# A two-batch encoder layer on one core: block products in another order, mixture tiles loaded by the sync engine, row splits behind the mixture, accumulating stores over two stages

## The chip, the cores and the metric

The kernel runs on one core of one Trainium2 chip. The core has a matrix engine (TensorE, in the profile PE, with its weight loads as PEld), a vector engine (VectorE, DVE), an activation engine (ScalarE, ACT), a general engine (GpSimd, POOL) and a sync engine (SyncE, SP) that here only issues transfers. GpSimd issues transfers as well. Each engine runs its own instructions strictly in the order in which they were written out for it, and each waits on semaphores for what the others and the transfers deliver. The metric is the device time of one execution in microseconds (us), as the median of the runs.

## The reference

One layer of an encoder is applied to two requests with the same weights: `x_prompt` with 1024 tokens (A in what follows) and `x_sample` with 512 tokens (B), 1024 wide.

```python
h = rms_norm(x, pre_w)
cols = jnp.einsum('bsd,dc->bsc', h, w_in)
m_qk, m_v, m_o, m_z, m_i, m_f, a_qkv, a_z, gate = jnp.split(cols, np.cumsum(IN_SPLITS)[:-1], axis=-1)
y_m = mlstm_mixer(m_qk, m_v, m_o, ...) * jax.nn.silu(m_z)
y_a = dilated_attention(a_qkv, rel_table) * jax.nn.silu(a_z)
p_m = jnp.einsum('bsc,cd->bsd', y_m, w_pm)
p_a = jnp.einsum('bsc,cd->bsd', y_a, w_pa)
g = jax.nn.sigmoid(gate).reshape(b_, s_, N_BRANCHES, D_MODEL)
merged = g[:, :, 0] * p_m + g[:, :, 1] * p_a
out = jnp.einsum('bsd,de->bse', merged, w_out)
return x + rms_norm(out, post_w)
```

`dilated_attention` computes three groups of windows and mixes them for every token and head by their softmax denominators. This is the mixture that the change speaks of:

```python
mx = jnp.stack(maxes)
w = jnp.exp(mx - jnp.max(mx, axis=0))
num = jnp.einsum('gbsh,gbshe->bshe', w, jnp.stack(outs))
den = jnp.sum(w * jnp.stack(dens), axis=0)
return (num / den[..., None]).reshape(b_, s_, A_WIDTH)
```

## The kernel before

All large products are in float32. Each operand is split into a rounded high part and the low part that is left (the high part by a copy on ScalarE, the low part by a subtraction on VectorE), and each product is three matmuls: high by high, low by high, high by low. That is `mm3` (L232 to L237), and its three lines are L235, L236 and L237. A split thus costs two instructions on two engines, and a matmul can start only when both halves are there.

**The first stage.** A's input projection uses one level of Strassen-Winograd: instead of eight block products, seven, on sums and differences of the blocks. `unit_pair` (L835) does this for a pair of units (a unit is 128 columns of the projection): the seven products `m1` to `m7` of twelve matmuls each, and between them copies on ScalarE and sums on VectorE. Every product has a bank of PSUM of its own (the pool hands out tiles named `d`), but for two: `m2` accumulates onto `m1`'s bank and `m3` onto `m5`'s. Before `m2` may start, ScalarE must have copied `m1` to `u2` (L854, in the trace `pu<-d`); before `m3` may start, ScalarE must have copied `m5` to `q[1][1]` (L863, in the trace `c<-d`). The sums of the weights' blocks are split into halves by `pair_split` (L762 to L769), high on ScalarE (L766), low on VectorE (L767), into the tiles `phla` and `phlb`; two of the splits, `s3, a22` and `s4`, are made inside `unit_pair`, and `s3` is the weight of `m7`.

**The middle.** Behind it come A's mLSTM and attention with the short pieces of B's projection woven in, then A's output (`outputs`). Its last stage does not add to the result in memory by itself: it puts 16 stores on a list `adds`; each is a transfer issued by GpSimd that accumulates onto `T.y` in memory (L2496, `y_prompt<-H`). B's attention (`attend`) runs at the end of this part; it writes its outputs with their maxima and denominators to `og` in memory.

**The tail** is about B alone. Five pieces take part, and TensorE's order there is the order in which they are written out: the mixture `combine` is a generator that is stepped between the steps of a `Fill`, which hands out weights and runs `branches` and then `final`.

- `combine` (L2066): the four tiles of 128 tokens go through two buffers, tiles 0 and 2 through `V0a`, tiles 1 and 3 through `V1a`. For each tile a load from `og` per group (three), then on VectorE `weigh` (L2081 to L2096, which gives the weights `cw`, with reciprocal L2094), three products `mix` (L2103) and two sums `add` (L2109); then `turn` (L2111): four transposes on TensorE (L2114) and a multiplication by `az` on VectorE (L2116). Tiles 0 to 2 are then stored to `ym` in memory; the last tile goes directly into the operands of `proj_a` (L2120). The loads of tiles 2 and 3 are issued by `ahead` on `self.side`, which is GpSimd's queue there, and stand behind `self.loaded`, the last load of weights.
- `split` (L2196): loads the four rows 8 to 11 of `ym` (tiles 0 to 2 side by side, 384 wide) through the three buffers `self.rows_in` (`ymr`, `ymr`, `sraw`), and splits each, high L2211 on ScalarE into `H`, low L2212 on VectorE into `K`. The fourth row uses the buffer of the first.
- `branches` (L2562): `proj_m` makes eight column tiles of eight steps of three matmuls, evicted by VectorE (L2593) into `V0b` and `V1b`, and issues the accumulating stores, two per column tile (L2583 to L2585); `proj_a` makes eight column tiles of four steps, and merges each with its `proj_m` tile (L2612 to L2615). It is `proj_a` that needs `H` and `K`.
- `final` (L2634): 192 matmuls with `w_out`. Its weights come through two buffers `wraw` (loaded by L288) and are split by L299 on ScalarE and L305 on VectorE into places that `more_places` adds to.
- `STEPS` and `fill.stage` set how many of the Fill's steps lie between two steps of `combine`.

**What sets the order.** TensorE's order in the tail, and SP's, is that of the code (`manual_schedule`). The order on VectorE, ScalarE and GpSimd is set by a scheduler at build time, which takes the instruction that its own timeline finds ready first. `issue_after(x.ins)` keeps an instruction behind `x` in that order, and `high_priority` pulls one ahead. The mixture's own VectorE steps have both (they stay behind the last eviction of `proj_m` and behind the sums of the tile before); `split`'s low parts have neither.

## Time and profile before

| | |
|---|---|
| runs (us) | 2201.39, 2202.01, 2204.64; median 2202.01 |
| the profiled execution (us) | 2203.76 |
| its span, first to last instruction (us) | 2202.0 |
| mean granted TensorE clock | 0.995 |
| moved by the transfers | 469.04 MB, mean 213 GB/s |
| matmuls | 11530 |

The profile is of one execution. A row of a group names the engine, the line of the code, the operation, the output and input tiles, and their shape; "x608" is the count. The busy time, the mean duration and the idle time that the engine spent ahead of these instructions follow, with what ended it. "PE tp <- DVE Q" reads: TensorE waited to write `tp` until VectorE had made `Q`. Rows of the timeline begin with the start in us from the span's beginning. Matmuls are pipelined: one takes 0.39 us or so from start to end, but the next starts 0.227 us after it, so that TensorE's busy time hides waits shorter than the overlap.

### The profile page before, as it was taken

The page shows a single profiled execution, that of the slowest core. Times are in us where ns is not written, and L with a number is a line of the kernel's source. Part 1 is how long each engine was busy: PE and PEld are TensorE (multiplying, and loading weights), DVE is VectorE, ACT ScalarE, POOL GpSimd, SP SyncE. Part 2 cuts the span into 40 slices and gives each one's busy share as a digit, 9 for nine tenths or more (in the row PEclk, how much of TensorE's full clock was granted, in tenths as well). Part 3 has the DMA queues.
Part 4 walks back from the last instruction along what each step waited for, and adds up shares of the span by engine and source line. Part 5 has one row for each costly group of instructions (what it writes and reads, how often), then busy time and mean ns, then how long its engine had stood idle before and what let it go on. Part 6 is the DMA issues. An engine that isn't in the chain of part 4 may idle for free.

```text
span 2202.0 us, 33824 instructions
## 1 busy us (share of the span) xinstructions
PE 2164.1 (98%) x11530; PEld 1840.2 (84%) x11530; DVE 1502.4 (68%) x2923; ACT 1122.2 (51%) x2324; POOL 808.2 (37%) x1050
## 2 busy tenths in 40 slices
PE   9999999999999999999999999999999999999978
PEld 8988888888888788888888889998788888888766
DVE  8766675668888776537888775574667846676844
ACT  7322354455444444446777666666755544435312
POOL 1000444333234775325776650011045532322431
PEclk9999999999999999999999999999999999999989
DMA  5642687955555554358646558877668788986873
GB/s 213 192 138 72 210 274 242 302 203 201 184 185 196 200 201 153 134 201 267 197 161 232 170 169 263 239 238 196 201 233 283 239 278 295 319 253 196 251 234 107
DMA packets 234134, 469.04 MB, mean 213 GB/s; under 512 B 38281, under 2 KB 120393, under 8 KB 233834
## 3 DMA queue, kind: packets, MB, share of 16 engines
q1 hardware_dynamic: 199736, 343.81, 47.8%
q0 software_dynamic: 30624, 110.48, 15.6%
q10 hardware_dynamic: 3602, 12.59, 1.4%
q8 instruction: 91, 1.49, 0.3%
q14 instruction: 81, 0.66, 0.1%
HBM read 314.56 MB, written 156.43 MB: 214 GB/s over the span
## 4 chain that ended last, share of the span: by engine, by line
PE 81%; DVE 5%; DMA 5%; issue 4%; ACT 3%; POOL 1%; DVEq 0%; SPq 0%; POOLq 0%; ACTq 0%
PE d L235 11%; PE dense L235 11%; PE d L237 11%; PE d L236 11%; PE dense L236 11%; PE dense L237 11%; PE lg L1851 2%; PE pt L1881 1%; DVE pwk L882 1%; PE o L1924 1%; PE num L235 1%; PE num L237 1%; PE num L236 1%; PE num L1544 1%; DMA wraw<-w_out 1%
## 5 line engine op out<-in xcount | busy, mean ns | idle before, releaser
L235 PE MATMUL dense<-H,wh 128*128 128x512 f32 x712 | 288.9, 406 | 0.0
L237 PE MATMUL dense<-H,wl 128*128 128x512 f32 x712 | 279.4, 392 | 0.0
L236 PE MATMUL dense<-H,wh 128*128 128x512 f32 x664 | 260.3, 392 | 0.0
L235 PE MATMUL d<-Hh,phla 128*128 128x512 f32 x608 | 237.7, 391 | 1.9 <-ACT pu L854 1.6
L237 PE MATMUL d<-Hh,phla 128*128 128x512 f32 x608 | 236.7, 389 | 0.0
L236 PE MATMUL d<-Hl,phla 128*128 128x512 f32 x608 | 236.6, 389 | 0.0
L235 PE MATMUL d<-Hh,phlb 128*128 128x512 f32 x456 | 177.8, 390 | 0.9 <-ACT c L863 0.9
L236 PE MATMUL d<-Hl,phlb 128*128 128x512 f32 x456 | 177.4, 389 | 0.0
L237 PE MATMUL d<-Hh,phlb 128*128 128x512 f32 x456 | 177.4, 389 | 0.0
L237 PEld LDWEIGHTS dense<-H,wl 128*128 128x128 f32 x712 | 134.0, 188 | 30.1
L235 PEld LDWEIGHTS dense<-H,wh 128*128 128x128 f32 x712 | 134.5, 189 | 18.0 <-issue 0.9
L305 DVE TENSOR_TENSOR wl<-wraw,wh 128x1024 fp32r<-128x1024 f32 (+1 forms) x96 | 120.0, 1252 | 30.2 <-ACT wh L299 30.1
L785 POOL TENSOR_TENSOR psum_w<-pw_raw 128x512 f32<-128x512 f32 x38 | 52.7, 1387 | 235.5 <-DMA pw_raw<-w_in 127.5
L235 PEld LDWEIGHTS d<-Hh,phla 128*128 128x128 f32 x608 | 114.1, 188 | 29.3 <-ACT pu L854 5.8
L1870 DVE CUSTOM_DVE_ANT_0 ls<-lg,bias 128x256 f32<-128x256 f32 (+2 forms) x240 | 78.6, 350 | 86.8 <-PE lg L1851 65.8
L236 PEld LDWEIGHTS dense<-H,wh 128*128 128x128 f32 x664 | 125.3, 189 | 14.5
L237 PEld LDWEIGHTS d<-Hh,phla 128*128 128x128 f32 x608 | 114.1, 188 | 23.9
L236 PEld LDWEIGHTS d<-Hl,phla 128*128 128x128 f32 x608 | 114.1, 188 | 23.4
L1874 ACT ACTIVATE ls<-ls,nm 128x256 f32<-128x256 f32 (+1 forms) x192 | 87.4, 456 | 77.4 <-DVE nm L1872 58.7
L299 ACT ACTIVATE wh<-wraw 128x1024 fp32r<-128x1024 f32 (+1 forms) x99 | 101.7, 1031 | 45.2 <-PE dense L236 23.4
L235 PE MATMUL d<-v,Hh 128*128 128x484 f32 (+1 forms) x336 | 121.3, 361 | 0.1
L237 PE MATMUL d<-v,Hl 128*128 128x484 f32 (+1 forms) x336 | 120.6, 359 | 0.4 <-DVE Hl L475 0.4
(749 smaller groups left out, 5936.2 us busy)
## 6 DMA issues: line engine op xcount, KB each, us to landing
pw_raw<-w_in SPq DMA_DIRECT2D x76, 512.0 KB, 4.6
wraw<-w_in SPq DMA_DIRECT2D x63, 512.0 KB, 4.7
pw_raw<-w_q SPq DMA_DIRECT2D x44, 512.0 KB, 6.5
pre<-phlb SPq DMA_DIRECT2D x32, 512.0 KB, 4.9
aqk_a<-pwk SPq DMA_DIRECT2D x32, 512.0 KB, 7.5
pre<-phlb SPq DMA_DIRECT2D x16, 1024.0 KB, 7.8
wh<-pre POOLq DMA_DIRECT2D x27, 512.0 KB, 6.4
wl<-pre POOLq DMA_DIRECT2D x27, 512.0 KB, 6.4
```

The costliest lines, as they stand in the source:

```text
L235: nc.tensor.matmul(out, lh, rh, start=start, stop=False, **kw)
L236: nc.tensor.matmul(out, lh, rl, start=False, stop=False, **kw)
L237: nc.tensor.matmul(out, ll, rh, start=False, stop=stop, **kw)
L299: high = nc.scalar.activation(hi[:, :n], raw[:, :n], AF.Copy)
L305: low = (self.lows or nc.vector).tensor_sub(lo[:, :n], raw[:, :n], hi[:, :n].bitcast(F32))
L785: self.nc.gpsimd.tensor_add(s[:, 0], ws[1][:, 0], ws[1][:, 1])
L882: nc.vector.scalar_tensor_tensor(y, raw[:, i:i + S], cw[:, i:i + 1], y, op0=OP.mult, op1=OP.add)
L1544: nc.tensor.matmul(pn, hi[:, j], z[:, c1], start=j == 0 and z is v[0], stop=False)
L1851: nc.tensor.matmul(lg[:, hh], q[hh][:, qs], z.rearrange("p (n j) -> p n j", j=P)[:, pair], start=z is k[hh], stop=z is not k[hh])
L1870: nc.vector.tensor_tensor_reduce(out=ls[rows, hh], in0=ts["lg"][hh][rows, of], in1=bt[rows, hh, by], scale=1.0, scalar=NEG, op0=OP.add, op ...
L1874: self.held = self.held[-3:] + [nc.scalar.activation(ls[:, hh], ls[:, hh], AF.Exp, bias=nm[:, hh:hh + 1], accum_out=ot[:, 128 + hh:129 + hh])]
L1881: nc.tensor.transpose(pp[:, hh * nk + x], ts["ls"][:, hh, x * P:(x + 1) * P], self.ident)
```

## The change

It has four parts.

1. In `unit_pair` the seven products come in another order: `m1, m6, m7, m5, m2, m4, m3` in place of `m1, m6, m2, m7, m5, m4, m3`. ScalarE's copy of `m5` is gone; VectorE adds `u3` and `m5` straight from PSUM. The priority of the copy `u2` is gone too.
2. In `combine` the loads of tiles 2 and 3 are issued by SP (the default of `fetch`) and no longer stand behind the last load of weights. `az` stays on GpSimd's queue. The last sum of each tile is also kept as `self.summed`; the first tile gets one more step, and the Fill's steps are dealt out by `STEPS` 20, 56 in place of 26, 50.
3. In `split` the low parts stand behind `self.summed`, the latest sum of the mixture when they are written out, which is that of the last tile.
4. In `branches` the sixteen accumulating stores are issued as follows: in `proj_m` two in each of the column tiles 0 and 1 and one in each of 2 to 5, in `proj_a` one in each of its eight. The extra places for split weights are added at column tile 0 of `proj_a` and not at 2, and they lie in `V0a` and `V1a` in place of `H0` and `H3`.

```diff
         m1 = product(B11, a11)
-        with self.tc.high_priority():
-            nc.scalar.activation(u2, m1, AF.Copy)
+        nc.scalar.activation(u2, m1, AF.Copy)
         m6 = product(T2, s2)
         nc.vector.tensor_add(u2, u2, m6)
-        m2 = product(B21, a12, m1)
-        nc.scalar.activation(q[0][0], m2, AF.Copy)
         m7 = product(T3, s3)
         nc.vector.tensor_sub(u3, u2, m7)
         m5 = product(T1, s1)
-        with self.tc.high_priority():
-            nc.scalar.activation(q[1][1], m5, AF.Copy)
-        nc.vector.tensor_add(q[1][1], q[1][1], u3)
+        nc.vector.tensor_add(q[1][1], u3, m5)
+        m2 = product(B21, a12, m1)
+        nc.scalar.activation(q[0][0], m2, AF.Copy)
         m4 = product(T4, a22)
...
         def ahead(t, g=None):
             if t < T.n:
+                if g is not None:
+                    self.fetch(("og", T.S), cs[t % 2][:, g], T.og[t * P:(t + 1) * P, g])
+                    return
                 with self.tc.issue_after(self.loaded.ins):
-                    if g is None:
-                        az[t] = az_of()
...
-                    else:
-                        self.fetch(("og", T.S), cs[t % 2][:, g], T.og[t * P:(t + 1) * P, g], self.side)
+                    az[t] = az_of()
...
                     if i == 5:
-                        summed = last
+                        summed = self.summed = last
...
                     yield
+                    if not t:
+                        yield
                     if t:
                         ahead(t + 1, 2)
...
                     nc.scalar.activation(hi[:, z, :w], t[:, :w], AF.Copy)
-                    nc.vector.tensor_sub(lo[:, z, :w], t[:, :w], hi[:, z, :w].bitcast(F32))
+                    with self.tc.issue_after(self.summed.ins):
+                        nc.vector.tensor_sub(lo[:, z, :w], t[:, :w], hi[:, z, :w].bitcast(F32))
...
+        def accumulate():
+            with self.tc.issue_after(self.loaded.ins):
+                self.adds.pop(0)()
...
-                    if k % 4 == 3 and self.adds:
-                        with self.tc.issue_after(self.loaded.ins):
-                            self.adds.pop(0)()
+                    if k == 3 and ct < 6 or k == 7 and ct < 2:
+                        accumulate()
...
-                if ct == 2:
-                    self.more_places(weights.__self__, [[z[:, 1024 * i:1024 * (i + 1)] for i in range(2)] for z in map(self.take, ("H0", "H3"))])
+                if ct == 0:
+                    self.more_places(weights.__self__, [[z[:, 1024 * i:1024 * (i + 1)] for i in range(2)] for z in map(self.take, ("V0a", "V1a"))])
+                accumulate()
                 pa = self.dense()
...
-STEPS = (316, 260, 192, (6.25, 4.75), 26, 50)
+STEPS = (316, 260, 192, (6.25, 4.75), 20, 56)
...
-                fill.stage(STEPS[5], 3 * B.n + 2)
+                fill.stage(STEPS[5], 3 * B.n + 3)
```

The first place is on VectorE, in the tail, where the last tile of the mixture is worked on. The rows L2094 and L2096 are the end of its weights `cw` (`wd` is the denominators' part), L2103 its products and L2109 its sums in `Q`, L2116 and L2120 what follows its turn, and L2212 the low parts of the rows of `split`. Before:

```order
L2094 RECIPROCAL wd_20671<-wd_20671 128x8
L2212 TENSOR_TENSOR K_20500<-ymr_17723,H_20499 128x384
L2096 SCALAR_TENSOR_TENSOR cw_20666<-cw_20666,wd_20671 128x24
L2212 TENSOR_TENSOR K_20500<-sraw,H_20499 128x384
L2103 TENSOR_TENSOR Q_20303<-V1a,cw_20666 128x512 x3
L2212 TENSOR_TENSOR K_20500<-ymr_17722,H_20499 128x384
L2109 TENSOR_TENSOR Q_20303<-Q_20303 128x512 x2
L2212 TENSOR_TENSOR K_20500<-ymr_17723,H_20499 128x384
L2116 TENSOR_TENSOR az_20298<-tp_20764,az_20298 128x512
L2120 TENSOR_TENSOR K_20500<-az_20298,H_20499 128x4x128
```

After, where the same steps stand at L2091, L2093, L2100, L2106, L2113 and L2117, and L2595 is the eviction of a column tile of `proj_m`:

```order
L2091 RECIPROCAL wd_20626<-wd_20626 128x8
L2093 SCALAR_TENSOR_TENSOR cw_20621<-cw_20621,wd_20626 128x24
L2100 TENSOR_TENSOR Q_20265<-V1a,cw_20621 128x512 x3
L2106 TENSOR_TENSOR Q_20265<-Q_20265 128x512
L2595 SCALAR_TENSOR_TENSOR V1b<-gab,dense 128x512
L2106 TENSOR_TENSOR Q_20265<-Q_20265 128x512
L2113 TENSOR_TENSOR az_20260<-tp_20723,az_20260 128x512
L2595 SCALAR_TENSOR_TENSOR V1b<-gab,dense 128x512
L2117 TENSOR_TENSOR K_20462<-az_20260,H_20461 128x4x128
L2212 TENSOR_TENSOR K_20462<-ymr_17685,H_20461 128x384
L2212 TENSOR_TENSOR K_20462<-sraw,H_20461 128x384
L2212 TENSOR_TENSOR K_20462<-ymr_17684,H_20461 128x384
```

The four low parts stood one ahead of each step of the last tile; now all four come behind its last step (the fourth is two rows further down), and an eviction stands between its two sums.

The second place is on GpSimd, where `proj_m` ends and `proj_a` begins. `y_prompt<-H` are the accumulating stores, `gab` the merge gates, `wh` and `wl` the weights of `proj_a` (split beforehand), `wraw<-w_out` the weights of `final`. Before:

```order
L2496 DMA y_prompt<-H_19609 128x512
L2496 DMA y_prompt<-H_20046 128x512
L276 DMA gab<-gt_b 128x512
L832 DMA wh_7389<-pre 128x1024
L832 DMA wl_7390<-pre 128x1024
L288 DMA wraw_7383<-w_out 128x1024
L288 DMA wraw_7384<-w_out 128x1024
L276 DMA gab<-gt_b 128x512 x3
L288 DMA wraw_7383<-w_out 128x1024
```

After:

```order
L832 DMA wh_7351<-pre 128x1024
L832 DMA wl_7352<-pre 128x1024
L288 DMA wraw_7345<-w_out 128x1024
L2496 DMA y_prompt<-H_19571 128x512
L2496 DMA y_prompt<-H_20008 128x512
L288 DMA wraw_7346<-w_out 128x1024
L276 DMA gab<-gt_b 128x512 x3
L288 DMA wraw_7345<-w_out 128x1024
L2496 DMA y_prompt<-H_19571 128x512
```

The last stores stood ahead of the weights of `proj_a` and of all loads of `w_out`; now eight of them stand among the loads of `w_out`, two ahead of a load. The loads `V0a<-og_b` and `V1a<-og_b`, three each, are no longer on GpSimd's list; they stand on SP's, behind the first tiles' loads and ahead of the first store `ym_b<-az`.

On TensorE the turns of tiles 0 and 1 stand six and three matmuls earlier among those of `proj_m`, and the turns of tiles 2 and 3 where they were. In the first stage ScalarE's list loses the 38 copies of L863.

More of the change, by code (lines that the diff above doesn't have):

```diff
@@ L2127, in ahead @@
             if t < T.n:
+                if g is not None:
+                    self.fetch(("og", T.S), cs[t % 2][:, g], T.og[t * P:(t + 1) * P, g])
+                    return
                 with self.tc.issue_after(self.loaded.ins):
-                    if g is None:
-                        az[t] = az_of()
-                        self.fetch(("az", T.S), az[t].rearrange("p (c s) -> p c s", c=4),
-                                   T.az[:, :, t * P:(t + 1) * P].rearrange("c p s -> p c s"), self.side)
-                    else:
-                        self.fetch(("og", T.S), cs[t % 2][:, g], T.og[t * P:(t + 1) * P, g], self.side)
+                    az[t] = az_of()
+                    self.fetch(("az", T.S), az[t].rearrange("p (c s) -> p c s", c=4),
+                               T.az[:, :, t * P:(t + 1) * P].rearrange("c p s -> p c s"), self.side)
         if slow:
@@ L2591, in proj_m @@
                     if k == KT - 1:
-                        assert ct < KT - 1 or not self.adds
                         self.evicted = nc.vector.scalar_tensor_tensor(m2[ct // 4][:, ct % 4], gates.pop((1, ct)), 1.0, pm, op0=OP.add, op1=OP.mult)
```

## The prediction

> **What bounds the kernel now.** I read the page first: its first part, and its two groups of matmuls of the first stage.
>
> ```profile
> span 2202.0 us, 33824 instructions
> PE 2164.1 (98%) x11530; PEld 1840.2 (84%) x11530; DVE 1502.4 (68%) x2923; ACT 1122.2 (51%) x2324; POOL 808.2 (37%) x1050
> L235 PE MATMUL d<-Hh,phla 128*128 128x512 f32 x608 | 237.7, 391 | 1.9 <-ACT pu L854 1.6
> L235 PE MATMUL d<-Hh,phlb 128*128 128x512 f32 x456 | 177.8, 390 | 0.9 <-ACT c L863 0.9
> ```
>
> TensorE works 2164.1 of 2202.0 us. No matmul is added or taken away, so the change can win only what TensorE waits, or what it runs slowly. Next I asked for the windows of the stages that the diff touches: the length, busy time per engine with counts in brackets, then granted clock, DMA share, GB/s.
>
> ```profile
> 232.00:962.00 730.00, 727.20 (x3194) 597.83 (x3193) 509.37 (x468) 353.35 (x412) 319.47 (x236) 1.00 0.59 202
> 2038.00:2126.00 88.00, 71.49 (x299) 57.62 (x299) 53.94 (x109) 19.68 (x38) 35.62 (x51) 0.90 0.81 229
> 2126.00:2148.00 22.00, 22.00 (x98) 18.12 (x97) 15.52 (x22) 7.62 (x10) 7.49 (x14) 1.00 0.83 279
> 2126.00:2202.00 76.00, 66.71 (x288) 53.48 (x286) 36.62 (x53) 18.49 (x32) 15.07 (x28) 0.97 0.46 157
> ```
>
> The first row is the stage of `unit_pair`: 2.8 us idle in 730. The second runs from B's last attention tile to the end of `proj_m`: 16.5 us idle in 88, clock 0.90. Here is the prize. The third is `proj_a`: not idle. In the fourth most idle time is the drain after the last matmul, which the diff leaves alone. What TensorE waited for in the second window, from the list of waits (total, times, longest):
>
> ```profile
> PE tp L2114 <- DVE Q L2109: 12.2, 1, 12.2
> PE tp L2114 <- DVE cw L2086: 2.2, 2, 2.0
> PE tp L2114 <- DVE X L2109: 2.1, 1, 2.1
> PE dense L235 <- ACT K L2614: 0.8, 1, 0.8
> ```
>
> All but the last are the transposes in `turn`, one set of four for each mixture tile 0 to 3, and the 12.2 us belong to tile 3. Why VectorE was late shows in its timeline (start, length, line, output and inputs, idle before and who ended it).
>
> ```profile
> 2075.31 1.89 DVE L2103 TENSOR_TENSOR Q<-V1a,cw 128x512 f32<-128x512 f32 x3
> 2087.45 0.68 DVE L2109 TENSOR_TENSOR X<-X 128x512 f32<-128x512 f32 x1
> 2094.47 0.17 DVE L2086 TENSOR_TENSOR cw<-V1a 128x8 f32<-128x8 f32 x1 [4.61 <-DMA V1a<-og_b]
> 2096.54 0.20 DVE L2094 RECIPROCAL wd<-wd 128x8 f32<-128x8 f32 x1
> 2105.37 0.56 DVE L2212 TENSOR_TENSOR K<-ymr,H 128x384 fp32r<-128x384 f32 x1 [8.63 <-ACT H L2211]
> 2106.41 1.89 DVE L2103 TENSOR_TENSOR Q<-V1a,cw 128x512 f32<-128x512 f32 x3
> ```
>
> Two delays are in series. Tile 3 is in V1a only at 2094.47. Then, with the weights all but done at 2096.74, VectorE's next instruction in order is a low part of `split` (L2212), whose row isn't there: it stands 8.63 us, and the last products of the mixture stand behind it. The chain says what that row waited for:
>
> ```profile
> 2089.89 7.07 DMA ym_b<-Q
> 2097.10 7.61 DMA ymr<-ym_b
> 2110.24 1.08 PE tp L2114 x4
> 2111.32 0.43 PE dense L235
> ```
>
> Tile 2's result goes to memory in 7.07 us and comes back as a row in 7.61. So tile 3 waits for a round trip of tile 2 that it does not need.
>
> **The mixture.** With `issue_after(self.summed.ins)` all four low parts come behind tile 3's sums on VectorE, as the order rows in the section on the change show. The 8.63 us go. The other delay is the load: POOL issued it late, behind accumulating stores and other loads.
>
> ```profile
> 2084.95 0.57 POOL L276 DMA_DIRECT2D V1a<-og_b  x1
> ```
>
> V1a was free at 2077.20, when tile 1's products ended (2075.31 + 1.89). SP has nothing queued there but the loads and stores of `ym`, so it will issue tile 3 as each group frees, from about 2076. The time from issue to landing is in the list of DMAs, 7.1 us for the same buffer issued by SP (last column):
>
> ```profile
> q0 software_dynamic: 8413, 25.56, 53.7%
> q1 hardware_dynamic: 4864, 5.83, 10.2%
> y_prompt<-H POOLq DMA_DIRECT2D x12, 256.0 KB, 7.9
> V1a<-og_b SPq DMA_DIRECT2D x3, 264.0 KB, 7.1
> wraw<-w_out POOLq DMA_DIRECT2D x8, 512.0 KB, 3.7
> ```
>
> So tile 3 lands by about 2084.3, ahead of tile 2's end on VectorE (2087.45 + 0.68 = 2088.13), and what VectorE does becomes the bound: weights 2.27 (2094.47 to 2096.74), products 1.89, two sums of 0.68, and two instructions that the new order puts between them, an eviction of `proj_m` and the multiplication after tile 2's turn, about 0.7 each. That is 2088.13 + 6.9 = 2095.0. TensorE gets to the turn at the end of the second row below:
>
> ```profile
> 2088.27 0.63 PE L2114 MATMUL tp<-ident,X 128*128 128x128 f32 x4 [2.08 <-DVE X L2109]
> 2097.66 0.39 PE L237 MATMUL dense<-K,wl 128*128 128x512 f32 x1
> 2116.22 0.40 PE L235 MATMUL dense<-H,wh 128*128 128x512 f32 x1
> ```
>
> 2098.05 is 3 us later than 2095.0: no wait is left, 12.2 us go. The other turns stay where they are: turns 0 and 1 move two and one steps ahead in TensorE's order, but what they wait for on VectorE (splits of weights, the stores' normalisations) moves no more than that; I take 0 for their 4.3 us, with all of it as the bound of gain.
>
> The idle time also cost speed. Two windows of the clock:
>
> ```profile
> 2088.00:2092.00 4.00, 3.73 (x12) 3.04 (x13) 1.86 (x3) 0.00 (x0) 1.08 (x2) 0.61 1.10 263
> 2110.00:2116.00 6.00, 5.76 (x16) 4.73 (x17) 2.63 (x5) 0.63 (x1) 2.24 (x5) 0.50 0.17 31
> ```
>
> After the long wait (second row) the clock is 0.50. The transposes took 1.08 instead of 0.63, and from 2111.32 to 2116.22 matmuls start 0.43 apart instead of 0.227 (19.04 us for 84, below): 4.9 us for what takes 2.6. 0.45 + 2.3 = 2.8 us, which go with the wait. Sum for the mixture: 12.2 + 2.8 = 15.0 us. The Trainium skill, page "TensorE: Matmul & The Clock Gate", section "Part 1: The HAM clock gate (the "warmup" mystery)", says that the clock halves after an idle window of about 3.4 us and is given back after about 3.4 us of work. By that alone the slow part would be worth 1.7 us and the sum 13.9; the trace has about 6 us at 0.50, and a dip to 0.61 after a wait of 2.08 that the rule would not throttle, so the rows decide.
>
> The four low parts now come later. The rows arrive at 2104.71 as before (2097.10 + 7.61), as no row shows tile 2's store coming sooner. Of the 342 matmuls behind turn 3, 288 are those of `proj_a` and `final`, so `proj_a` needs the rows after 54: 2098.05 + 0.6 + 54 x 0.227 = 2110.9, and the fourth row 9 matmuls later, at 2113.0. This row's buffer holds the first row until its split has read it, to about 2105.9; a second load of 7.61 and 1.1 for the two halves end at 2114.6, 1.6 too late. But the share of the DMA engines was 0.17 from 2110 on (second row above). I take 0, with 1.6 as the bound.
>
> **The first stage.** Per pair of units seven products of twelve matmuls. Before, the third product goes onto the first one's bank and so waits for the copy u2 (L854), and the seventh onto the fifth's, waiting for the copy at L863. After, four products lie between m1 and m2 on one bank; m5's bank has two products between, and its reader is VectorE. What these waits cost is measured by the products' starts:
>
> ```profile
> 231.99 0.40 PE L235 MATMUL d<-Hh,phla 128*128 128x512 f32 x1
> 719.68 0.50 PE L235 MATMUL d<-Hh,phla 128*128 128x512 f32 x1 [1.57 <-ACT pu L854]
> 771.50 0.39 PE L235 MATMUL d<-Hh,phla 128*128 128x512 f32 x1
> 790.54 0.39 PE L235 MATMUL d<-Hh,phla 128*128 128x512 f32 x1
> 961.68 0.39 PE L237 MATMUL d<-Hh,phlb 128*128 128x512 f32 x1
> ```
>
> An undisturbed pair takes 790.54 - 771.50 = 19.04. There are 38 ((608 + 456) / 28). The stage took 961.91 - 231.99 = 729.9, 6.4 more than 38 x 19.04 = 723.5. That is the most that can be had; the idle columns show only 2.8 of it, since matmuls overlap. It does not all come: at 719.68, the worst, m7 takes the waiting product's slot at 718.1, but its weights are split only at 718.90:
>
> ```profile
> 716.97 1.93 DVE L767 TENSOR_TENSOR phlb<-pw_raw,phlb 128x1024 fp32r<-128x1024 f32 x1
> ```
>
> That leaves 0.8 there, and other pairs have 1 to 3 us to spare for the same split, which moves 2.7 nearer. VectorE's copy of m5 must follow m7's difference, in a stage where VectorE is 70% busy. I take 4.0, with 0 and 6.4 as ends. The 38 copies of L863 that ScalarE no longer makes are worth nothing by themselves: it is busy 353 of 730.
>
> **The accumulating stores.** Sixteen stay. Eight leave `proj_m` for `proj_a`, and there each pair stands in POOL's queue ahead of a load of w_out. Their price in DMA time: in the tail (162 us) the queue of SP took 10.2%, 16.5 us for 5.83 MB, or 2.83 per MB; POOL's took 53.7%, 87.0 us for 25.56 MB. Without the sixteen stores (4.2 MB) that is 21.4 MB, 60.5 us at SP's rate; the rest is 26.5, 1.7 us a store. In `proj_a` the engines had 0.83 x 22 = 18.3 us of work; eight stores more are 13.6, and 10 us of it would be left at its end. Against it, V0a and V1a are given as places for split weights two column tiles sooner, and B's last projection wants its weights over the 44 us of its 192 matmuls, not at once. What TensorE waits there now for the merged rows, whose instructions stand on VectorE between the splits of w_out, is 0.8. So the cost lies between -0.8 and 10, and I take 1.0, by the row of 0.8, as the third window is full in spite of its share of 0.83.
>
> Sum: 15.0 + 4.0 - 1.0 = 18.0 us. The profiled execution took 2203.76 with a span of 2202.0; the median of the runs is 2202.01, so the execution was 0.1% above it, and I subtract from the median: 2184.
>
> **Rivals.** *The transfers set the end.* The engines run full here (share 1.10 at 2088), so tile 3 might land at 2094.47 whoever issues it. Then its sums end at 2094.47 + 2.27 + 1.89 + 1.36 + 0.7 = 2100.7, a wait of 2.7, a dip of the clock like that of 2088 (4 us at 0.61, 1.6), and the rows' 1.6: 5.9 us back, 2190. For it: the share. Against it: 7.1 from issue to landing in the same stretch, and half of the stores gone. The Trainium skill, page "DMA: Bandwidth & Descriptors", section "Issuing engines are not separate DMA queues", says that transfers run on the same sixteen engines whoever issues them, and that another issuer saves only the time of issuing. By it the move to SP brings only the 8 us between 2076 and 2084.95 in which POOL had not issued; which is the term used above.
>
> *The first stage gains nothing*, as the split of m7's weights or m5's reader takes the copies' place in the pairs that waited: 2184 + 4 = 2188.
>
> *The stores hold back w_out*: slower. The sixth load of w_out lands now 24.5 us after `proj_a`'s start at 2126.0:
>
> ```profile
> 2147.12 3.38 DMA wraw<-w_out
> ```
>
> If POOL's queue is served strictly in turn, it stands behind eight stores at 7.9 / 2 = 4 us each (two overlap) and lands with six loads at 3.7 after 32 + 22 = 54 us, and the last projection waits the 30 us between: 2183 + 30 = 2213. It decides from the point where a store costs 3.2 us of the queue: 8 x 3.2 + 22 - 24.5 = 23 us eat the 19 won and 4 more. By the shares it is 1.7.
>
> *No change*: tile 3's turn waits as long for something that no row here shows, 2202.
>
> **Numbers.** Forecast 0.62, transfers 0.15, first stage without gain 0.15, stores 0.04, no change 0.04. A measurement of this kernel can tell about 0.2%, 4.4 us. All but the last two are faster by more: 0.92, 0.04, 0.04. Range: best case 6.4 + 15.0 + 4.3 + 0 = 26, 2176; the other end is the transfers' case with half of the first stage's gain lost and 2 more for the stores, 2194, which also takes in the first stage without gain and stores at 7 of their 10.
>
> **What would show it.** Right: no wait of PE for L2109 above 3 us and clock 1.00 from 2092 on; L2212 behind tile 3's sums on VectorE; V1a's loads on SP; no wait of PE for `pu` or `c` before 962 and the stage about 4 us shorter. Wrong: PE waiting for K or H at `proj_a`'s start, for w_out splits or for the merged rows in B's last projection, or for phlb in the first stage.

## The result

| | before | after |
|---|---|---|
| median of the runs (us) | 2203.22 (2201.39 to 2204.64) | 2185.37 (2184.17 to 2188.97) |
| ratio, with its 95% interval | | 0.9922 (0.9905 to 0.9939) |
| span of the profiled execution (us) | 2202.0 | 2183.2 |
| mean granted clock | 0.995 | 0.999 |

The change wins 17.85 us in the medians and 18.8 in the spans; 2184.0 was forecast. Of all executions in this document one, of the kernel with the copy kept, ran at a mean granted clock of 0.753 and took 2670.1 us; it counts in that kernel's median (2184.39 without it) and not in its ratio. First the page of the changed kernel, its first part and the two groups that head the products of the first stage.

```profile
span 2183.2 us, 33774 instructions
PE 2158.5 (99%) x11530; PEld 1841.1 (84%) x11530; DVE 1496.9 (69%) x2923; ACT 1105.9 (51%) x2286; POOL 786.4 (36%) x1044
L235 PE MATMUL d<-Hh,phla 128*128 128x512 f32 x608 | 236.5, 389 | 0.0
L235 PE MATMUL d<-Hh,phlb 128*128 128x512 f32 x456 | 177.6, 390 | 0.2 <-DVE c L859 0.2
```

The matmuls are the same, 38 instructions of ScalarE are gone, and the waits for ScalarE's copies (1.9 and 0.9) with them. The windows of the tail say where the rest came from, and that some of it was given back (length, busy time by engine with counts, clock, share of the transfer engines, GB/s).

```profile
2038.00:2126.00 88.00, 84.95 (x379) 69.33 (x378) 63.98 (x123) 25.29 (x44) 37.81 (x56) 1.00 0.89 269
2136.00:2140.00 4.00, 3.52 (x9) 2.79 (x10) 1.12 (x2) 0.69 (x2) 3.72 (x7) 0.57 0.66 216
```

In the first window TensorE now stands 3.0 us and not 16.5, at clock 1.00 and not 0.90; since the work comes sooner, the window now also holds the second projection. The second window lies in B's last projection. There the clock is low, in a place where it had been 1.00. The list of TensorE's waits, of the whole tail (total, times, longest), shows both sides:

```profile
PE tp L2111 <- DVE cw L2083: 3.0, 2, 2.2
PE dense L235 <- ACT K L2617: 2.6, 1, 2.6
PE dense L237 <- DVE Q L2618: 1.0, 2, 0.6
```

The 12.2 us at the last turn are gone; new are 2.6 and 1.0 for the merged rows in B's last projection, where 0.8 and 0.2 stood. VectorE's timeline around the last tile (L2083 the beginning of the weights, L2100 products, L2106 sums, L2212 the last of the rows' low parts):

```profile
2082.66 0.16 DVE L2083 TENSOR_TENSOR cw<-V1a 128x8 f32<-128x8 f32 x1
2085.23 1.90 DVE L2100 TENSOR_TENSOR Q<-V1a,cw 128x512 f32<-128x512 f32 x3
2088.24 0.69 DVE L2106 TENSOR_TENSOR Q<-Q 128x512 f32<-128x512 f32 x1
2101.45 0.56 DVE L2212 TENSOR_TENSOR K<-ymr,H 128x384 fp32r<-128x384 f32 x1 [2.05 <-ACT H L2210]
```

VectorE takes up tile 3 (first row) without a wait for its load. Its sums end at 2088.93, and all four low parts follow. TensorE's rows of the places that the prediction speaks of, from the first stage's first and last product to the last matmul:

```profile
232.33 0.40 PE L235 MATMUL d<-Hh,phla 128*128 128x512 f32 x1
957.13 0.39 PE L237 MATMUL d<-Hh,phlb 128*128 128x512 f32 x1
2082.89 0.63 PE L2111 MATMUL tp<-ident,X 128*128 128x128 f32 x4 [0.83 <-DVE cw L2083]
2090.92 0.60 PE L2111 MATMUL tp<-ident,Q 128*128 128x128 f32 x4
2103.65 0.40 PE L235 MATMUL dense<-H,sw 128*128 128x512 f32 x1
2132.05 0.50 PE L237 MATMUL dense<-wh,Q 128*128 128x512 f32 x1 [0.38 <-DVE Q L2618]
2135.14 0.50 PE L235 MATMUL dense<-wh,K 128*128 128x512 f32 x1 [2.59 <-ACT K L2617]
2136.49 0.79 PE L237 MATMUL dense<-wh,Q 128*128 128x512 f32 x1 [0.61 <-DVE Q L2618]
2175.01 0.39 PE L237 MATMUL dense<-V1a,Q 128*128 128x512 f32 x1
```

Cut at these places, with the rows of before (the last matmul of before starts at 2193.30), the 18.8 us of the spans fall into: ahead of the first stage 0.3 lost (231.99 to 232.33); the first stage 729.9 to 725.0, 4.9 won; from there to the third turn 1126.4 to 1125.5, 0.8 won; from the third to the last turn 22.0 to 8.0, 13.9 won; from the last turn to the last matmul 83.1 to 84.1, 1.0 lost; behind it 0.5 won. The last stretch is the interesting one. After the last turn no matmul should have to run cold any more, which alone is worth 2.8; yet the stretch got longer.

### The profile page after: what moved, and what is told of

It reads as the page before. It is cut to its first block, busy times and chain, and to the rows that moved or that the text cites. A ratio compares the mean times of both kernels' runs of the same rounds, so it can differ in the third digit from the quotient of the medians.

```text
span 2183.2 us, 33774 instructions
## 1 busy us (share of the span) xinstructions
PE 2158.5 (99%) x11530; PEld 1841.1 (84%) x11530; DVE 1496.9 (69%) x2923; ACT 1105.9 (51%) x2286; POOL 786.4 (36%) x1044
## 5 line engine op out<-in xcount | busy, mean ns | idle before, releaser
L1867 DVE CUSTOM_DVE_ANT_0 ls<-lg,bias 128x256 f32<-128x256 f32 (+2 forms) x240 | 78.7, 351 | 90.5 <-PE lg L1848 65.9
L236 PEld LDWEIGHTS dense<-H,wh 128*128 128x128 f32 x664 | 125.3, 189 | 14.5
L299 ACT ACTIVATE wh<-wraw 128x1024 fp32r<-128x1024 f32 (+1 forms) x99 | 101.8, 1032 | 50.7 <-PE dense L236 30.6
```

Source lines behind the costliest of these rows:

```text
L236: nc.tensor.matmul(out, lh, rl, start=False, stop=False, **kw)
L299: high = nc.scalar.activation(hi[:, :n], raw[:, :n], AF.Copy)
L1867: nc.vector.tensor_tensor_reduce(out=ls[rows, hh], in0=ts["lg"][hh][rows, of], in1=bt[rows, hh, by], scale=1.0, scalar=NEG, op0=OP.add, op ...
```

## The experiments

The table has the median in us, and from each kernel's profile three lengths, measured as above: the first stage, TensorE's wait at the last turn, and the stretch from the last turn to the last matmul.

| kernel | median | first stage | wait, last turn | last turn to last matmul |
|---|---|---|---|---|
| before | 2203.2 | 729.9 | 12.2 | 83.1 |
| changed | 2185.4 | 725.0 | 0 | 84.1 |
| changed, once more | 2185.4 | 724.8 | 0 | 86.2 |
| before, first stage alone | 2185.5 | 724.2 | 0 | 86.0 |
| before, first stage, later load | 2185.4 | 724.4 | 0 | 86.5 |
| before, load alone | 2196.6 | 730.7 | 9.7 | 82.5 |
| before, low parts alone | 2193.7 | 729.8 | 2.1 | 82.6 |
| before, load and low parts | 2190.6 | 729.7 | 0 | 86.7 |
| changed, old first stage | 2191.5 | 730.1 | 0 | 84.2 |
| changed, stores back | 2186.6 | 723.9 | 0 | 83.1 |
| changed, half the stores | 2178.2 | 724.1 | 0 | 78.7 |
| changed, gates by SyncE | 2185.5 | 724.9 | 0 | 87.1 |
| changed, copy kept | 2185.0 | 723.8 | 0 | 85.2 |
| changed, stores late | 2178.3 | 725.1 | 0 | 78.2 |

Between profiles of kernels with the same first stage its length spreads by about 1 us; the last column spreads by 2 us for the changed kernel itself. Most of that is the clock: in this stretch the first profile's trace has 3.41 us at a clock of 0.50, the second's 6.83, which costs 1.7 more. The last section says what decides between the two.

### The parts one by one, on the kernel before

**The first stage alone** (the hunk of `unit_pair` in the change, nothing else).

> The kernel before with the new order of the block products alone. Theory (the two banks' copies cost TensorE the time between products): the first stage loses 4.5 to 5 us of its 729.9 and the whole run as much, 2203.2 - 4.7 = 2198.5; the tail still waits 12 us at the last turn. Rival (the order only moves waits to the splits of the weights or into later stages): the stage is shorter, but the run by less than 2 us. Rival (the tail's timing hangs on the first stage's end): the run moves by more than 7 us.

It took 2185.54, a ratio of 0.9925 (0.991 to 0.994): all that the whole change wins, and 13 us more than the theory said. The third expectation was met in its number. The list of waits in the tail says how:

```profile
PE dense L235 <- ACT K L2611: 2.3, 2, 1.9
PE dense L237 <- DVE Q L2612: 2.1, 2, 1.2
PE tp L2111 <- DVE cw L2083: 2.0, 1, 2.0
```

The wait of the last turn is gone here too, though nothing in the mixture was edited. The order on VectorE, ScalarE and GpSimd is made by a scheduler with a timeline of its own, and that edit changed the order; so the cause is not the end of the first stage as such. On GpSimd the loads of tile 3 now stand ahead of a load of weights, two of `az` and four stores, on VectorE the low parts behind the sums of tile 3. GpSimd's and VectorE's rows of this kernel:

```profile
2070.45 1.22 POOL L276 DMA_DIRECT2D V1a<-og_b  x2
```

```profile
2087.34 1.41 DVE L2106 TENSOR_TENSOR Q<-Q 128x512 f32<-128x512 f32 x2
2096.81 0.56 DVE L2209 TENSOR_TENSOR K<-ymr,H 128x384 fp32r<-128x384 f32 x1 [8.06 <-ACT H L2208]
```

The load is issued 14.5 us sooner than before (2084.95), and VectorE still stands 8.06 us for the first row, but now behind the sums, where TensorE does not wait for it.

**The load alone.**

```diff
             if t < T.n:
+                if g is not None:
+                    self.fetch(("og", T.S), cs[t % 2][:, g], T.og[t * P:(t + 1) * P, g])
+                    return
                 with self.tc.issue_after(self.loaded.ins):
...
```

> The kernel before with the loads of mixture tiles 2 and 3 on SyncE alone; the low parts of the rows may stand where the scheduler puts them, which now is behind the first of the last tile's two sums instead of ahead of its weights. Theory (two delays in series, and the row's is the later one): the low part of the first row, ahead of the last sum, still ends only when tile 2 has come back from memory, so the last turn still waits 6 to 9 us of the 12.2; gain 3 to 6 us, 2197 to 2200. Rival (the load was the whole delay): the wait at the last turn goes, gain 14 to 18 us, 2185 to 2189. Rival (the load did not matter): gain under 1 us.

It took 2196.56, a ratio of 0.9969 (0.9958 to 0.9981), 6.7 us won, with a wait of 9.7. The two-delays theory holds, with sizes a bit above its ranges. VectorE's rows show the mechanism undisguised:

```profile
2086.48 0.16 DVE L2086 TENSOR_TENSOR cw<-V1a 128x8 f32<-128x8 f32 x1
2092.49 0.68 DVE L2109 TENSOR_TENSOR Q<-Q 128x512 f32<-128x512 f32 x1
2102.84 0.56 DVE L2212 TENSOR_TENSOR K<-ymr,H 128x384 fp32r<-128x384 f32 x1 [9.67 <-ACT H L2211]
2103.79 0.68 DVE L2109 TENSOR_TENSOR Q<-Q 128x512 f32<-128x512 f32 x1
```

Tile 3 is there at 2086.48, 8 us sooner than before. But the low part of the first row is between the two sums, and the second sum, which the turn needs, stands 9.67 us behind it.

**The low parts alone.**

```diff
-                        summed = last
+                        summed = self.summed = last
...
-                    nc.vector.tensor_sub(lo[:, z, :w], t[:, :w], hi[:, z, :w].bitcast(F32))
+                    with self.tc.issue_after(self.summed.ins):
+                        nc.vector.tensor_sub(lo[:, z, :w], t[:, :w], hi[:, z, :w].bitcast(F32))
```

> The kernel before with the low parts of the rows behind the last tile's sums alone; the loads stay on GpSimd's queue. Theory (two delays in series): tile 3 still lands at about 2094.5, its sums end at about 2100.7, the last turn waits about 2.7 us with a dip of the clock of about 1.6; gain 15.0 - 4.3 = 10.7 us, 2192.5. Rival (the row was the whole delay): gain 15 us or more, 2188 or less. Rival (the row only stood behind the load): gain under 4 us.

It took 2193.72, a ratio of 0.9956 (0.9939 to 0.9973): 9.6 us in the medians against 10.7 expected, and a wait of 2.1 against 2.7. Here the load is what is late:

```profile
2092.89 0.17 DVE L2086 TENSOR_TENSOR cw<-V1a 128x8 f32<-128x8 f32 x1 [4.42 <-DMA V1a<-og_b]
```

So of the 12.2 us the low parts' place decides over 10, and the load over the last 2.

**Both** (the two diffs above together, stores and steps as before).

> The kernel before with both parts of the mixture's change, the accumulating stores and the steps as before. Theory (the two together remove the wait of the last turn, and the stores in the middle do not hinder the loads): gain 15 to 18 us, 2185 to 2188, and no more than 1 us of waits of TensorE in B's last projection. Rival (the sixteen stores in the projection ahead hold back loads, which the change of the stores mends): gain 10 to 13 us, with TensorE waiting at a turn or for a row at the second projection's start.

The waits of the turns are down to the first one's 2.0, but the run took 2190.55, a ratio of 0.9944 (0.9929 to 0.9959): 12.7 us, short of the 15 to 18. The theory missed; the rival's 10 to 13 was met in the number and not in the place. No later turn and no row made TensorE wait, but its waits behind the last turn were 3.9 us in place of 1.0:

```profile
PE dense L237 <- DVE Q L2616: 2.0, 2, 1.5
PE tp L2114 <- DVE cw L2086: 2.0, 1, 2.0
PE dense L235 <- DVE mg L2613: 1.1, 1, 1.1
PE dense L235 <- ACT K L2615: 0.8, 1, 0.8
```

The stores are all in the first projection in this kernel, and still the last stretch takes 86.7. What is given back behind the turn is therefore not the price of spreading the stores. (3.4 of the 86.7 are again the clock, 6.83 us at 0.50.)

**The first stage with a later load** (besides the first stage's edit; `self.added` is the store issued last, and the loads of tile 3 stand behind it).

```diff
...
                 elif i == 6:
                     ahead(t)
                     yield
+                    if t == 2:
+                        for g in range(3):
+                            ahead(3, g)
```

> The kernel before with the new order of the block products, and the loads of the last mixture tile put three transfers later on GpSimd's list than where that edit alone put them (behind a load of weights, one of az and a store; the kernel before has three more transfers and a store ahead). Theory (what the first stage's edit gave in the tail is the earlier place of these loads on GpSimd's list, 2070.5 in place of 2085.0): the loads are issued at about 2076.5 and land 4 to 5 us later, the last turn waits 3 to 4 us, with a dip of the clock behind it; 2190, 4 to 5 us slower than with the first stage's edit alone (2185.5). Rival (it was only the place of the low parts on VectorE, which stays behind the sums here): 2185.5 within 1.5.

It took 2185.41, a ratio of 0.9918 (0.99 to 0.9936), with no wait at the last turn, which is the rival's time. But the kernel moved the loads less than meant: they were issued at 2072.9 to 2075.7, 2.4 to 3.8 us later than with the first stage's edit alone. VectorE waited 0.31 us for tile 3 at 2081.94, and the sums were still done 1.9 us ahead of the turn (2089.49 for 2091.39). So the run doesn't decide between the two places. What does is the pair above: load alone 9.7 us left, low parts alone 2.1. The third turn waits 2.5 us in this profile, which was taken of the slowest of its four executions (2188.31).

### The parts taken back, on the changed kernel

**The old first stage** (the products in the old order, all else as changed).

> The changed kernel with the first stage's products in the old order. Theory (the mixture's edits work by themselves; the first stage is worth its own 4.9 us and no more): the stage takes 729.9, the last turn waits under 1 us, the run 2185.4 + 4.9 = 2190.3. Rival (the order of the tail hangs on the scheduler's timeline, so that any edit may turn it): another order on VectorE or GpSimd and a time more than 3 us off 2190.3, to either side.

It took 2191.53, a ratio of 0.9947 (0.9932 to 0.9962): 6.2 us more than the changed kernel, with a first stage of 730.1 and no wait at the last turn. So the mixture's edits hold by themselves, and the first stage is worth its own length. Over all profiles that is 730.0 (five with the old order, the kernel before among them) against 724.5 (nine with the new one), 5.6 us.

This kernel and the one with load and low parts differ only in the stores, the places for split weights and the Fill's steps. Their times are 2191.5 and 2190.6, with ratios of 0.9947 and 0.9944 whose intervals overlap: those three together are worth nothing that these runs can show, and none was run alone but the stores.

**The copy kept.**

```diff
-        nc.vector.tensor_add(q[1][1], u3, m5)
+        nc.scalar.activation(q[1][1], m5, AF.Copy)
+        nc.vector.tensor_add(q[1][1], q[1][1], u3)
```

> The changed kernel with the new order of the products, but with ScalarE's copy of the fifth product kept, to which VectorE then adds. Theory (the order does it: two products lie between the fifth and the one on its bank): the first stage takes 724 to 725 us as in the changed kernel, the run 2185.4 within 1.5. Rival (ScalarE, freed of 38 copies, splits the weights sooner, and that is the gain): the stage takes 727 us or more, the run 2188.

2184.95, a ratio of 0.9917 (0.9904 to 0.9931), and a first stage of 723.8. It is the order of the products; the 38 copies are free either way.

**The stores back in the first projection.**

```diff
-                    if k == 3 and ct < 6 or k == 7 and ct < 2:
+                    if k % 4 == 3 and self.adds:
                         accumulate()
...
-                accumulate()
                 pa = self.dense()
```

> The changed kernel with all sixteen accumulating stores in the first projection again, the places for split weights as changed. The prediction's term (eight stores in the second projection cost 1.0 us): 1 us faster than the changed kernel, 2184.4, the waits of TensorE behind the last turn down from 3.6 to about 1 us. Theory after the first four kernels (spreading the stores gains, since the kernel with the stores as before took 86.7 us from the last turn to the last matmul and the changed one 84.1): 2 us slower, 2187.5, with 86 to 87 us on that stretch.

2186.61, a ratio of 0.9924 (0.9909 to 0.9939). The interval holds the changed kernel's 0.9922, so the times don't tell the two apart. The profile has 2.3 us of waits behind the last turn, where the prediction's term expected about 1, and 83.1 for the last stretch, 1.0 and 3.1 less than the changed kernel's two profiles and not the 86 to 87 of the other theory. On the other side the third turn waits 1.9 and not 0.8. The spreading itself is worth nothing that these runs can show.

**Half the stores.**

```diff
-                accumulate()
+                self.adds.pop(0)
                 pa = self.dense()
```

> The changed kernel with the eight accumulating stores of the second projection left out (half of the last stage's sums for the first request are then missing from its output). Theory (what is given back behind the last turn is transfers: gates and weights that land late because the stores use the same engines): the waits behind the last turn fall from 3.6 to under 1.5 us and the run to 2181 to 2182. Rival (it is VectorE, where splits of w_out stand ahead of the merged rows): no change over 1 us, 2185.

2178.21, a ratio of 0.9888 (0.9873 to 0.9903), 7.2 us less than the changed kernel, and more than expected. TensorE waits for nothing behind the last turn, and the stretch takes 78.7, 5.4 less; some 1.7 of the rest lie ahead of the tail, where the first stage ended sooner. From 2090 to 2150 the gates land in 5.1 us and not 7.4, the loads of `w_out` in 3.8 and not 6.2. Two windows of 22 us from the start of the second projection, of the changed kernel and of this one:

```profile
2103.00:2125.00 22.00, 22.00 (x98) 18.12 (x97) 13.41 (x19) 5.78 (x8) 13.83 (x21) 1.00 0.97 277
2125.00:2147.00 22.00, 18.43 (x72) 14.15 (x71) 10.99 (x15) 6.24 (x11) 5.40 (x11) 0.92 0.69 220
```

```profile
2102.00:2124.00 22.00, 22.00 (x98) 18.12 (x97) 17.18 (x24) 8.60 (x11) 7.46 (x14) 1.00 0.73 260
2124.00:2146.00 22.00, 21.98 (x95) 17.43 (x95) 9.95 (x13) 6.40 (x11) 4.24 (x8) 1.00 0.37 129
```

The shares of the transfer engines fall from 0.97 and 0.69 to 0.73 and 0.37: (0.24 + 0.32) x 22 = 12.3 us of engine time for eight stores, an estimate of 1.5 each. TensorE pays 5.4 for them in this pair of profiles.

**The gates by SyncE** (`None` is SyncE's queue, and `br == 0` the second projection).

```diff
-                self.fetch(("gt", T.S, br, ct), g, T.gt[br, ct, :, b * BLK:(b + 1) * BLK], self.side)
+                self.fetch(("gt", T.S, br, ct), g, T.gt[br, ct, :, b * BLK:(b + 1) * BLK], None if br == 0 else self.side)
```

> The changed kernel with the gates of the second projection loaded by SyncE, which has nothing else to do there, and not by GpSimd behind stores and weights. Theory (the last gate is late because of its place in GpSimd's queue): the wait of 2.6 us for the last merged rows goes and with it the dip of the clock of about 1.4; 2181 to 2182. Rival (the transfers share the engines, so another issuer lands no sooner): the gate still takes 7 to 8 us and TensorE waits as long; 2185. Rival (the low parts of w_out on VectorE): as the second.

2185.51, a ratio of 0.9919 (0.9903 to 0.9936), no gain. The list of transfers (last column: us from issue to landing), of the changed kernel and of this one, from 2090 to 2150:

```profile
wraw<-w_out POOLq DMA_DIRECT2D x8, 512.0 KB, 6.2
gab<-gt_b POOLq DMA_DIRECT2D x8, 256.0 KB, 7.4
```

```profile
wraw<-w_out POOLq DMA_DIRECT2D x8, 512.0 KB, 6.6
gab<-gt_b SPq DMA_DIRECT2D x8, 256.0 KB, 6.8
```

The gates land 0.6 us sooner, the weights 0.4 later, and TensorE waits 5.4 us in B's last projection. That transfers share the same engines whoever issues them is what the Trainium skill says, page "DMA: Bandwidth & Descriptors", section "Issuing engines are not separate DMA queues"; these rows agree. Both rivals had 2185, so the time doesn't tell them apart. The rows of what makes the merged rows do, first of the changed kernel (the last gate) and then of this one (L299 splits a load of `w_out`, L2617 copies a merged row):

```profile
2132.30 0.69 DVE L2615 SCALAR_TENSOR_TENSOR mg<-gab,dense 128x512 f32<-128x512 f32 x1 [0.30 <-DMA gab<-gt_b]
```

```profile
2132.12 1.06 ACT L299 ACTIVATE wh<-wraw 128x1024 fp32r<-128x1024 f32 x1 [3.84 <-DMA wraw<-w_out]
2133.08 0.61 ACT L2617 ACTIVATE K<-mg 128x512 fp32r<-128x512 f32 x1
```

In the changed kernel the last gate was only 0.30 us late for VectorE. With the gates on SyncE none is, but ScalarE stands 3.84 us for a load of `w_out`, and the copy that TensorE waits for stands behind that load's split; its sum was done at 2130.55. So a late gate is not the whole delay: the loads of `w_out` are late as well, and their splits stand ahead of the merged rows, as the last rival said.

**The stores late.** If the engines are what is short, the stores belong where they are idle.

```diff
-                accumulate()
                 pa = self.dense()
...
                     for k in (2 * kp, 2 * kp + 1):
...
+                        if k == KT - 1 and i in (1, 2, 3, 4):
+                            for _ in range(2):
+                                accumulate()
```

> The changed kernel with the eight stores of the second projection issued in B's last projection instead, two each behind its first tiles 1 to 4, with all loads of w_out but one ahead of them. Theory (the stores cost 5.4 us because they share the engines with gates and w_out; the engines are at a share of 0.29 in the last 50 us): from the last turn to the last matmul 79 to 80 us in place of 84.1, the run 4 to 5 us faster than the changed kernel, 2181. Rival (they then hold back the loads of x_sample behind them, which the closing instructions need): TensorE is done sooner, but the end is no more than 1 us sooner, 2184.5 or more.

2178.31, a ratio of 0.9888 (0.9874 to 0.9901): as fast as without these stores, and 7.1 us faster than the changed kernel measured beside it (below), where 4 to 5 were expected. This version beats both kernels. TensorE's last turn and last matmul, and the window of its second projection:

```profile
2088.72 0.60 PE L2111 MATMUL tp<-ident,Q 128*128 128x128 f32 x4
2166.87 0.39 PE L237 MATMUL dense<-V1a,Q 128*128 128x512 f32 x1
```

```profile
2101.00:2123.00 22.00, 22.00 (x98) 18.11 (x97) 17.36 (x25) 8.47 (x12) 7.45 (x14) 1.00 0.76 265
2123.00:2145.00 22.00, 22.00 (x98) 17.98 (x97) 10.32 (x13) 6.48 (x12) 11.64 (x16) 1.00 0.95 228
```

78.15 us lie between the two rows; 342 matmuls at 0.227 are 77.6. The engines are just as full, at 0.95, but in the second window: GpSimd issues the first of these stores at 2124.92, behind all gates and seven of the eight loads of `w_out`, and TensorE is busy 22.00 of 22.

**The changed kernel once more.**

> The changed kernel once more, beside the two others: 2185.4, the first stage 724 to 725 us, 84 us from the last turn to the last matmul.

2185.42, a ratio of 0.9919 (0.9905 to 0.9932). The first stage is as expected, the last stretch at 86.2 is 2 us longer than in the first profile, 0.4 by longer waits (4.0 for 3.6) and 1.7 by the clock.

## Why the prediction was right, and where it was wrong

**The first stage: right.** 4.0 was forecast of at most 6.4; 4.9 came in the two profiles, 5.6 over all. What is left is what the step named, the split of `m7`'s weights and the reader of `m5`:

```profile
PE d L237 <- DVE phlb L767: 0.4, 1, 0.4
PE d L235 <- DVE c L859: 0.2, 1, 0.2
```

It was taken too low: that list has one wait for the split in 38 pairs, so the pair that was looked at was not a typical one. The copies were worth nothing by themselves, as said.

**The mixture: right for this change, with the two delays as described.** 15.0 was forecast. From the third turn to the last came 13.9, which is the wait of 12.2 and the dip of the clock to 0.61 behind the third turn, 1.6. With the cold matmuls behind the last turn (2.8) and 0.8 ahead of the third turn it is 17.5. The other turns' 4.3 were taken at 0; the third turn's wait fell from 2.1 to 0.8, and the dip behind it, though shown, had not been counted. Whether a wait of 2 us has such a dip is luck (last section), so 1.6 of the 17.5 need not come in every execution. The sums of tile 3 were to end 3 us ahead of TensorE; they ended at 2088.93, 2 us ahead. The load was there when VectorE came to it: SP issued it at 2070.04, 6 us sooner than forecast. (From 2076 to 2084.95 are 9 us, not the 8 of the rival; nothing hangs on it.)

**Not seen: the parts are not independent.** The prediction added the first stage and the mixture as two terms. For the whole change this holds: the first stage's own 5.6 and the 12.7 of the mixture's two edits make 18.3. But the wait of the last turn could also be removed by the scheduler's own choice, and the first stage's edit alone made that choice: 17.7 for it alone and 12.7 make 30.4, for a change that wins 17.85. So the time of the whole change is no proof of the mixture's part; the kernel with the old first stage is. That the edit moved the scheduler's timeline is read from its lists; why the timeline gave this order was not tried.

**The step "no row shows tile 2's store coming sooner": wrong, without consequence.** In the changed kernel the store to memory took 2.2 us and the row's load 2.9, where 7.07 and 7.61 stood; the trace lists them so:

```profile
ymr<-ym_b SPq DMA_DIRECT2D x3, 192.0 KB, 2.9
ym_b<-Q SPq DMA_DIRECT2D x1, 256.0 KB, 2.2
```

The fourth low part was done at 2102.0, ahead of the second projection's start at 2103.65, so no row made TensorE wait.

**The accumulating stores: the term that was mis-sized.** "I take 1.0, by the row of 0.8": the shared engines' price of a store was about right (1.7 worked out, 1.5 measured), and that much of it would be left over at the end of the second projection was right too (10 of 13.6 us forecast; 0.32 x 22 = 7.0 of 12.3 measured). The step failed in letting nearly all of it vanish in B's last projection. TensorE waited 3.6 us for merged rows, held up by gates (7.4 us to land) and by the splits of late loads of `w_out` (6.2), and then ran at half clock for 3.41 us, 1.7 more: 5.3 of the 5.4 that go when the stores are left out. In the kernel before the same stretch was 83.1 - 78.7 = 4.4 above that of the kernel without them, 2.8 of it the cold matmuls behind the turn; 1.6 is left, and 5.4 - 1.6 = 3.8 is the term in this profile, not 1.0; by the same sum it is 5.9 in the second profile of the changed kernel. Its cause was also put wrongly. The spreading is not to blame, since the stores in their old place give as much back (2.8 with the stores back, 6.4 with load and low parts). TensorE comes to the second projection 22 us earlier (2103.65 for 2126.0), and the same bytes have so much less time to land; this last is argued from the lengths, while the runs without these stores and with late ones show that it is the stores that cost. The rival that ends slower, the stores taking the queue strictly in turn at 3.2 us and more, did not come about: they cost 1.5 of the engines' time.

The sum was 15.0 + 4.0 - 1.0 = 18.0; the pieces were 17.5 + 4.9 - 3.8 = 18.6, and 0.2 at the two ends of the span together. It came out well since two gains that were taken too low paid for a cost that was taken too low. That much of the closeness of 2184.0 to 2185.4 is luck. The rival "the transfers set the end" was right about where the shortage was, though not about tile 3, which landed in time; its 5.9 us given back came in another stage, at about two thirds of the size.

## What to carry to other kernels

When a wait ahead of a stage goes, price the stage behind it with the transfers it needs and the time that is now left for them, not with the waits that it shows while it is protected; here 3.8 of 18 us went back in one profile and 5.9 in another. Stores that nobody waits for belong where the share of the transfer engines is low, which here was worth 7.1 us more, while issuing the gates from another engine was worth nothing. Where a scheduler orders the engines, an edit far away can remove a wait (or make one): compare the lists of all engines before an effect is put down to the edit beside it.

## What was not expected of the hardware

An accumulating store of 256 KB takes about 1.5 us of the time of all sixteen transfer engines, by the estimate above.

A wait of about 2 us left the clock alone at one turn and not at another: at the first turn 2.21 us were followed by 1.00 in the changed kernel, and 2.08 at the third turn of the kernel before by 0.61. The traces say what decides. Wherever one of the fourteen has a low clock (0.50) between the first 14 us and the last matmul, it lasts 3.41, 6.83, 10.24 or 13.65 us, always a multiple of 3.41. So within an execution the clock changes on a grid of 3.41 us, and against the kernel's work the grid lies elsewhere in each execution. Here are two steps of it around the first turn, of the changed kernel and of its second profile:

```profile
2061.24:2064.65 3.41, 1.65 (x8) 1.03 (x6) 3.09 (x5) 0.53 (x1) 3.41 (x6) 1.00 1.03 193
2064.65:2068.06 3.41, 2.96 (x15) 2.57 (x16) 3.12 (x11) 0.22 (x1) 3.41 (x6) 1.00 1.09 277
```

```profile
2059.95:2063.36 3.41, 1.41 (x9) 0.98 (x8) 3.22 (x7) 0.00 (x0) 3.41 (x7) 1.00 1.03 177
2063.36:2066.77 3.41, 3.41 (x10) 2.63 (x9) 2.18 (x8) 0.22 (x1) 3.08 (x5) 0.50 1.07 300
```

In the first the wait of 2.21 us falls across the edge of a step, which has 1.76 us idle, and the clock stays. In the second a shorter wait, 2.00, lies whole in one step, and the next step runs at 0.50. Laid out like this over all fourteen traces, each of the 20 steps at full clock with 1.90 us idle or more was followed by a step at 0.50, and none with 1.77 or less; in between are two, one with the dip (1.78) and one without (1.89). What counts is the idle time in a step and not the length of a wait. So a wait of 2 us costs 1.7 us of clock on top in some executions and nothing in others, and two profiles can differ by that much with nothing changed.
